# HGRN2 on one Trainium2 core: units paired by feature tile instead of by token half, and started earlier in the projection

## The chip, the cores and the metric

The kernel runs on one core of one Trainium2 chip. The metric is the device time of one execution in microseconds (us), the median of several runs. The engines are TensorE (PE in the rows), VectorE (DVE), ScalarE (ACT) and GpSimd (POOL); SyncE (SP) issues most DMAs.

## What is computed

Two layers of a decoder trunk on 1024 tokens of 1024 features, in fp32. In each layer one input projection feeds four head groups of 256 features each, two of which matter here:

```python
proj = rmsnorm(h, attn_norm_g[i]) @ w_in[i]
y_c = hgrn2_group(hg_q, hg_f, hg_i, lb_all[i])     # gated linear recurrence
y_d = s5_group(s5_u, ...)                          # state space, then a GLU

# hgrn2_group, per head and chunk of tokens
log_f = logaddexp(log(lb), log1p(-lb) + log_sigmoid(z)); k = (1 - lb) * sigmoid(-z)
bcum  = cumsum(log_f)
scores[t, s] = sum_k q[t, k] * k[s, k] * exp(bcum[t, k] - bcum[s, k])     # s <= t
o     = scores @ v + (q * exp(bcum)) @ state
state = exp(b_last) * state + (k * exp(b_last - bcum)).T @ v
```

The other two groups are attention. The groups are normalised, HGRN2's is gated, one output projection and a conv MLP follow.

## The kernel before

Features lie on the 128 partitions, tokens on the free axis in two halves of 512. A 256-feature group is thus two feature tiles (`ft`) by two token halves (`n`). Products in fp32 are made of three matmuls of split operands (`mm3`: L738, L739, L740 in the projection, L726 to L728 elsewhere). A weight tile is split by a cast (L714, ACT or DVE) and a subtraction (L103, DVE or POOL).

**HGRN2** is done in four units (`hgrn_unit`, L256), one for each feature tile and token half, of 15 steps each. A unit makes gates from `z` (L213: ACT's Abs, Exp and Ln, then on DVE `hk` L222, `z` L227, the running sum `hb` L237; in layer 1 also L230, L235, L236), then `kh` (L267, L269), which PE transposes (`khT`, L292). PE makes `pu` (L301) from the transposed `kT` and the values `v`, and DVE adds it to the running state `st` (L306, L308). Then seven levels follow. A level makes `g` (DVE L279, ACT exponentials, DVE L282) and two halves of `qz` (DVE L286); PE makes the scores `psc` (L327), and DVE puts them into `sc` under a mask (L331, L333). An eighth step writes the diagonal (PE L337, DVE L338). At the end PE makes `poh` from `sc`, `v`, `st` and `qb` (L351, L353), and ACT copies it to `yc` (L355). The state runs from token half 0 to token half 1 of one feature tile.

**S5** (`s5`) takes its two feature tiles in turn: DVE, POOL and ACT make matrices (`care`, `caim`, `bare`, `baim`), PE makes `ucp`, `utp` and `sin`, DVE the scans `s5z` (L585 to L609), then PE 24 matmuls into `ys` (L619, L622), and from `ys` come `yt` and the transposed `yf` (L635) and `yl`. A GLU follows: DVE's `zh` (L662), PE's `gl` (L726 to L728), DVE's `gs`, `gt` (L134, L135) and `yd` (L676).

**The projection** (`in_proj`) makes tile after tile in the order uf and z (ahead of the stage), hq, v, z, hq, misc, fq, fk, v, fq, fk, hg, hg, cq, cq, ckv. Each tile takes 8 x 3 matmuls for each token half, with an eviction on DVE (L1533, L1534, L1587) that multiplies by the norm's factor.

**The order.** `weave` (L684) steps generators in turn: each has a count of steps and a span of the stage, and the one whose next step is due earliest goes first. The projection spans 0 to 1, `s5` 0.1 to 0.7, `hgrn` the pair of numbers that is changed here. `hgrn` waits for flags that the projection sets: `h0` when the tiles of feature tile 0 are issued (z, hq, v), `h1` when those of feature tile 1 are. What `weave` issues is then laid on each engine's in-order queue by the tile framework's scheduler, so that the diff alone does not tell where an instruction stands.

Of the kernel before, what the change touches and what calls it, by code (L numbers as in the profile page):

```python
# [38 lines left out]

T = dict(early=(0, 0.2), s5=((0.1, 0.7), (0.1, 0.7)), hgrn=((0.35, 0.92), (0.35, 0.92)), cd=((0.05, 0.85), (0.05, 0.85)), prep=((0.3, 1), (0.3, 1)), b=(0, 1), a=(0.9, 0.95), pre=(7, 9, 11, 13), vals=(5, 6), ahead=3, plv=4, mx=0, pw=1, rt=2, sc=2, rp=6, dl=4, qk=(4, 4), up=5)


class Kern:
# [210 lines left out]
def hgrn_unit(K, layer, ft, n, z, q, v, lbc, st, y):  # L256
# [55 lines left out]
    for li in range(len(LEVELS) + 1):  # L312
        if li < len(LEVELS):
            g, qz = ahead
        if li == T['qk'][layer]:
            qk = K.h(name="qk")
# [491 lines left out]
def rms_steps(K, tiles, gains, out, gates=None):  # L808

    nc = K.nc  # L810
    V = nc.vector
    new = [[] for _ in tiles]
    out.extend(new)
    nm = Norm(K, gains, P * len(tiles), split=False)
    for n in range(2):
        for i, x in enumerate(tiles):
            nm.add(i, n, x[n])
        yield
        nm.scale(n)
        yield  # L820
        for i, x in enumerate(tiles):
            xn, hi, lo = K.h(name="xn"), K.h(F32R, "yh"), K.h(F32R, "yl")
            V.scalar_tensor_tensor(xn, x[n], gains[:, i:i + 1], nm.r(n), op0=ALU.mult, op1=ALU.mult)
            if gates is not None:
                V.tensor_tensor(xn, xn, gates[i][n], op=ALU.mult)
            nc.scalar.copy(hi, xn)
            K.lo(V if i % 2 else nc.gpsimd, lo, xn, hi)
            new[i].append((hi, lo))
        yield
# [39 lines left out]
class Head:  # L869
# [67 lines left out]

    def out(self, ahead=T['ahead']):

# [22 lines left out]
        for qh, kt in [(0, kt) for kt in range(4)] + [(1, kt) for kt in range(8)]:  # L962
# [11 lines left out]
            nc.scalar.activation(pr[:, 0:n], ps[:, 0:n], AF.Exp)  # L974
            K.lo(V if T['plv'] and kt % T['plv'] == T['plv'] - 1 else nc.gpsimd, pl[:, 0:n], pr[:, 0:n], ph[:, 0:n])
            pend.append((qh, kt, n, ph, pl))
# [8 lines left out]
def attention(heads):  # L985
# [13 lines left out]
    for i in range(len(heads)):  # L999
        nxt, pre = get(i + 2), iter(())  # L1000
        mx, vals = (b.max(), b.values()) if b else (iter(()), iter(()))
        for step, _ in enumerate(a.out()):
            for _ in range(2 if step % 2 or step < T['mx'] else 1):
                next(mx, None)
            if step == 6 and nxt:
# [3 lines left out]
                pre = nxt.prep()  # L1009
            if step in T['pre']:  # L1010
                next(pre, None)
            if step in T['vals']:
                next(vals, None)
# [438 lines left out]
def body(ctx, tc, xT, pT, pos, invf, sgn, vecs, prms, dsk, bfs, w_fm, w_misc, w_tm, w_uq, w_ukv, w_glu,  # L1452
         w_outb, w_up, w_down, w_pg, w_ple, out):
    nc = tc.nc
    K = Kern(tc, ctx)
# [45 lines left out]
    steps, lbc = [], K.const([P, 6], F32, "lbc")  # L1501
    ready = {}

    def early():

        for l in range(DEPTH):
            head = K.sm([P, 24], name="s5h", tag="s5h", bufs=2)
            nc.scalar.dma_start(head, prms[l][:, 0:24])
            steps.append(s5_steps(K, head))
            yield  # L1510
        rope_tables(K, pos, cst, tabs)
        K.exp_ln()
        hgrn_lb(K, vec[0][:, V_LB:V_LB + 4], lbc)
        ready["steps"] = True
        yield
        for _ in hgrn_consts(K):
            yield
        ready["consts"] = True
# [3 lines left out]
    for l in range(DEPTH):  # L1522
# [5 lines left out]
        z, hq, hv, hg, fq, fk, fv, misc, cq = ([] for _ in range(9))  # L1528
# [11 lines left out]
        rt = K.sm([P, 8], name="rt", tag="rt", bufs=2)  # L1540
# [57 lines left out]
        yc, yd = [K.two(name="yc") for _ in range(2)], []  # L1598
        yb, ya = ([K.two(name=n) for _ in range(2)] for n in ("yb", "ya"))
        h, ycs, yds, res, heads = [], [], [], {}, []  # L1600
# [11 lines left out]

        def hgrn():
            st = [K.h(name="st") for _ in range(2)]
            while "h1" not in ready or "consts" not in ready:
                yield
            for n in range(2):
                u = [hgrn_unit(K, l, ft, n, z[ft][n], hq[ft][n], hv, lbc, st[ft], yc[ft]) for ft in range(2)]
                for _ in range(HGRN_STEPS):
                    for g in u:  # L1620
                        next(g, None)
                        yield
            while "gates" not in ready:
                yield
            yield from rms_steps(K, yc, gain(2), ycs, gates=hg)
# [18 lines left out]

        pre = [(early(), 12, *T['early'])] if l == 0 else []
        weave(*pre, (s5(), 2 * S5_STEPS + GLU_STEPS + RMS_STEPS, *T['s5'][l]), (hgrn(), 4 * HGRN_STEPS + RMS_STEPS, *T['hgrn'][l]), (in_proj(), IN_STEPS, 0, 1))

        ready["fox"] = True
# [106 lines left out]
        xs, rp = nm.xs, nm.r  # L1755
# [6 lines left out]
        ws, pend, pw = {}, None, {}  # L1762
# [7 lines left out]
        for i, u in enumerate(units + [None]):  # L1770
# [3 lines left out]
            if pend:  # L1774
                n, m, c, v, t = pend
                V.scalar_tensor_tensor(t[:, c], v[:, c], 0.0, t[:, c], op0=ALU.min, op1=ALU.subtract)
                nc.scalar.activation(v[:, c], t[:, c], AF.Exp)
            if u:
                n, m, c = u
# [20 lines left out]
            if pend:  # L1800
                n, m, c, v, t = pend
# [101 lines left out]
```

## Time and profile before

| | |
|---|---|
| median of 3 runs | 3041.83 us (3039.55 to 3045.96) |
| profiled execution, its own time | 3032.95 us |
| its span | 3031.2 us |
| its mean granted TensorE clock | 0.958 of full speed |
| busy in the span | PE 93%, DVE 73%, ACT 47%, POOL 35% |
| projection of layer 0, first hq eviction to last ckv eviction | 62.7 to 426.5 us |
| projection of layer 1 | 1569.6 to 1912.1 us |

All times inside a run are from the profiled execution, in us from the start of its span. A clock of 1.00 in the profile's rows is 2.4 GHz and 0.50 is 1.2 GHz; a share between them is a stretch that held both.

### The profile page before, as it was taken

To read this page: it belongs to the slowest core of one execution; us is meant where nothing else is said; L and a number is where in the kernel's file an instruction comes from. 1 tells how busy PE (TensorE), PEld (TensorE's weight loads), DVE (VectorE), ACT (ScalarE), POOL (GpSimd) and SP (SyncE) were. 2 spreads that over 40 slices of the span, in tenths; PEclk is the share of its full clock that TensorE was granted. 3 is DMA by queue.
4 is the path that set the end of the run, shared out by engine and by line. 5 is a ranking of instruction groups with operands and counts; after the bars stand their busy time and mean duration, and the time that the engine had idled before them with its cause. 6 is when DMAs were issued, how large, how long until landed. Compare 5 with 4: busy or idle time off the path is not lost.

```text
span 3031.2 us, 37112 instructions
## 1 busy us (share of the span) xinstructions
PE 2825.1 (93%) x13346; PEld 2271.9 (75%) x13346; DVE 2208.3 (73%) x3254; ACT 1414.8 (47%) x2383; POOL 1068.9 (35%) x927
## 2 busy tenths in 40 slices
PE   7899799889899999999999888988989999999997
PEld 6777676666688888888787866766767888888886
DVE  6595768777999998242854966878699999953458
ACT  4234446665444444242732453657654444443346
POOL 2521013345422224555523210325453222255544
PEclk9898799899999999999999998999999999999998
DMA  3101011103222225352421010110032222263533
GB/s 125 38 15 49 22 59 35 35 1 132 70 83 84 84 84 172 130 191 92 152 88 36 19 56 28 53 56 1 31 123 90 82 82 82 82 212 98 185 107 129
DMA packets 112136, 249.68 MB, mean 82 GB/s; under 512 B 17488, under 2 KB 20176, under 8 KB 111952
## 3 DMA queue, kind: packets, MB, share of 16 engines
q1 hardware_dynamic: 110512, 246.66, 24.6%
q8 instruction: 105, 1.72, 0.2%
q10 hardware_dynamic: 1440, 0.65, 0.1%
q14 instruction: 79, 0.65, 0.1%
HBM read 197.58 MB, written 48.50 MB: 81 GB/s over the span
## 4 chain that ended last, share of the span: by engine, by line
PE 56%; DVE 21%; issue 7%; ACT 4%; POOL 2%; DMA 1%; SPq 0%; DVEq 0%; POOLq 0%; ACTq 0%
PE up L1320 8%; PE up L1319 8%; PE up L1318 8%; PE dn L1439 5%; PE dn L1440 5%; PE dn L1438 5%; DVE wx L103 1%; PE qk L968 1%; PE pj L738 1%; DVE mx L897 1%; DVE xq L1199 1%; PE pj L739 1%; PE ob L726 1%; PE pj L740 1%; PE ob L727 1%
## 5 line engine op out<-in xcount | busy, mean ns | idle before, releaser
L103 POOL TENSOR_TENSOR wx<-wr,wx 128x512 fp32r<-128x512 f32 (+1 forms) x293 | 485.6, 1670 | 362.2 <-ACT wx L1421 198.1
L1318 PE MATMUL up<-bh,wx 128*128 128x512 f32 x1232 | 482.8, 392 | 12.2 <-ACT wx L1311 12.2
L1319 PE MATMUL up<-bl,wx 128*128 128x512 f32 x1232 | 483.2, 392 | 7.0 <-DVE bl L103 4.0
L1320 PE MATMUL up<-bh,wx 128*128 128x512 f32 x1232 | 483.4, 392 | 6.3 <-DVE wx L103 6.3
L1318 PEld LDWEIGHTS up<-bh,wx 128*128 128x128 f32 x1232 | 233.5, 190 | 61.5 <-ACT wx L1311 13.1
L1439 PE MATMUL dn<-g,wx 128*128 128x512 f32 x704 | 274.1, 389 | 3.8 <-DVE g L103 3.8
L1319 PEld LDWEIGHTS up<-bl,wx 128*128 128x128 f32 x1232 | 233.5, 190 | 57.5 <-DVE bl L103 4.9
L1320 PEld LDWEIGHTS up<-bh,wx 128*128 128x128 f32 x1232 | 233.3, 189 | 56.9 <-DVE wx L103 8.3
L103 POOL TENSOR_TENSOR pl<-pr,ph 128x512 fp32r<-128x512 f32 x144 | 166.2, 1166 | 306.9 <-ACT pr L974 188.2
L1440 PE MATMUL dn<-g,wx 128*128 128x512 f32 x704 | 273.9, 389 | 0.0
L1438 PE MATMUL dn<-g,wx 128*128 128x512 f32 x704 | 273.9, 389 | 0.0
L103 DVE TENSOR_TENSOR g<-g,g 128x512 fp32r<-128x512 f32 x88 | 105.6, 1215 | 202.7 <-ACT g L1420 186.0
L103 POOL TENSOR_TENSOR wx<-wq,wx 128x512 fp32r<-128x512 f32 x44 | 65.1, 1479 | 517.5 <-ACT wx L1311 517.5
L738 PE MATMUL pj<-xs,wx 128*128 128x512 f32 (+1 forms) x512 | 212.3, 415 | 16.4 <-ACT xs L765 7.3
L1421 ACT CAST wx<-wr 128x1024 fp32r<-128x1024 f32 x88 | 92.4, 1050 | 277.9 <-PE dn L1439 255.4
L740 PE MATMUL pj<-xs,wx 128*128 128x512 f32 (+1 forms) x512 | 207.1, 405 | 2.5 <-DVE wx L103 2.5
L739 PE MATMUL pj<-xs,wx 128*128 128x512 f32 (+1 forms) x512 | 208.1, 406 | 1.1 <-DVE xs L766 1.1
L1439 PEld LDWEIGHTS dn<-g,wx 128*128 128x128 f32 x704 | 132.1, 188 | 32.1 <-DVE g L103 4.7
L1440 PEld LDWEIGHTS dn<-g,wx 128*128 128x128 f32 x704 | 132.1, 188 | 27.4
L1438 PEld LDWEIGHTS dn<-g,wx 128*128 128x128 f32 x704 | 132.1, 188 | 27.4
L1329 DVE SCALAR_TENSOR_TENSOR cv<-u,vec,cv 128x1023 f32<-128x1023 f32 x88 | 131.0, 1491 | 28.0 <-ACT cv L1328 27.8
L1330 DVE SCALAR_TENSOR_TENSOR cv<-u,vec,cv 128x1022 f32<-128x1022 f32 x88 | 137.8, 1568 | 0.1
(468 smaller groups left out, 6940.5 us busy)
## 6 DMA issues: line engine op xcount, KB each, us to landing
wr<-in_w_down SPq DMA_DIRECT2D x88, 512.0 KB, 3.5
wr<-in_w_up SPq DMA_DIRECT2D x88, 256.0 KB, 2.9
wq<-in_w_up SPq DMA_DIRECT2D x88, 256.0 KB, 3.9
hid<-cv SPq DMA_DIRECT2D x44, 512.0 KB, 3.3
g<-hid SPq DMA_DIRECT2D x88, 256.0 KB, 5.2
wr<-in_w_fm SPq DMA_DIRECT2D x30, 512.0 KB, 3.9
wr<-in_w_pg SPq DMA_DIRECT2D x28, 512.0 KB, 3.5
hdr<-h SPq DMA_DIRECT2D x48, 256.0 KB, 2.0
```

Source lines behind the costliest of these rows:

```text
L103: eng.tensor_tensor(out, x, hi.bitcast(F32), op=ALU.subtract)
L738: nc.tensor.matmul(out, lhsT=ah, rhs=bh, start=(i == 0), stop=False)
L739: nc.tensor.matmul(out, lhsT=ah, rhs=bl, start=False, stop=False)
L740: nc.tensor.matmul(out, lhsT=al, rhs=bh, start=False, stop=(i == n - 1))
L1318: nc.tensor.matmul(ps, lhsT=ah, rhs=bh, start=k == 0, stop=False)
L1319: nc.tensor.matmul(ps, lhsT=ah, rhs=bl, start=False, stop=False)
L1320: nc.tensor.matmul(ps, lhsT=al, rhs=bh, start=False, stop=k == KD // 2 - 1)
L1329: V.scalar_tensor_tensor(c[:, 1:], u[:, :S - 1], cw[:, 1:2], c[:, 1:], op0=ALU.mult, op1=ALU.add)
L1330: V.scalar_tensor_tensor(c[:, 2:], u[:, :S - 2], cw[:, 0:1], c[:, 2:], op0=ALU.mult, op1=ALU.add)
L1438: nc.tensor.matmul(ps[m], lhsT=ah, rhs=gh, start=f == 0, stop=False)
L1439: nc.tensor.matmul(ps[m], lhsT=ah, rhs=gl, start=False, stop=False)
L1440: nc.tensor.matmul(ps[m], lhsT=al, rhs=gh, start=False, stop=f == NFF - 1)
```

## The change

The loops over token halves and feature tiles inside `hgrn` change places. Before, the first pair of units was token half 0 of both feature tiles and the second pair was token half 1 of both. Now the first pair is both token halves of feature tile 0, which needs the flag `h0` only, and the second pair both halves of feature tile 1. The start of `hgrn`'s span goes from 0.35 to 0.2 in both layers; its end stays at 0.92.

```diff
-T = dict(..., hgrn=((0.35, 0.92), (0.35, 0.92)), ...)
+T = dict(..., hgrn=((0.2, 0.92), (0.2, 0.92)), ...)
...
         def hgrn():
             st = [K.h(name="st") for _ in range(2)]
-            while "h1" not in ready or "consts" not in ready:
-                yield
-            for n in range(2):
-                u = [hgrn_unit(K, l, ft, n, z[ft][n], hq[ft][n], hv, lbc, st[ft], yc[ft]) for ft in range(2)]
+            for ft in range(2):
+                while f"h{ft}" not in ready or "consts" not in ready:
+                    yield
+                u = [hgrn_unit(K, l, ft, n, z[ft][n], hq[ft][n], hv, lbc, st[ft], yc[ft]) for n in range(2)]
                 for _ in range(HGRN_STEPS):
                     for g in u:
                         next(g, None)
                         yield
```

The units and their instructions are the same. What moves is their place on the engines' queues. Three places are shown.

The first is DVE's queue in layer 0 behind the eviction of z's second token half. The numbers at the names are the tiles' own, which differ between the two programs; z_230 and z_231 are the two halves of feature tile 0. Before, the scans of the first S5 tile come next:

```order
L1533 TENSOR_TENSOR z_1044<-pj_1139,rs_344 128x512
L103 TENSOR_TENSOR wx_1507<-wr_1504,wx_1506 128x1024
L585 TENSOR_TENSOR s5z_1242<-sin_1224,phr_1091 128x512
...
L607 TENSOR_TENSOR s5z_1245<-s5z_1245,s5z_1244 128x4x127
L609 TENSOR_TENSOR s5z_1246<-s5z_1246,s5z_1243 128x4x127
L1533 TENSOR_TENSOR hq_1204<-pj_1279,rs_344 128x512
L103 TENSOR_TENSOR wx_1718<-wr_1715,wx_1717 128x1024
L1534 TENSOR_TENSOR misc_1337<-pj_1345,rs_260 68x512
```

Now the first pair's gates, `kh`, two levels of each unit and the state's first copy stand there:

```order
L1533 TENSOR_TENSOR z_1044<-pj_1147,rs_344 128x512
L222 SCALAR_TENSOR_TENSOR hk_1142<-z_230,ha_1141 128x512
L227 SCALAR_TENSOR_TENSOR z_230<-z_230,ha_1141 128x512
...
L237 SCALAR_TENSOR_TENSOR hb_1186<-anew,z_231 128x512
L585 TENSOR_TENSOR s5z_1264<-sin_1246,phr_1091 128x512
...
L609 TENSOR_TENSOR s5z_1268<-s5z_1268,s5z_1265 128x4x127
L267 TENSOR_TENSOR kh_1307<-hb_1186 128x512
...
L286 SCALAR_TENSOR_TENSOR qz_1353<-g_1348,heads,hq_488 128x256 x2
L1533 TENSOR_TENSOR hq_1226<-pj_1313,rs_344 128x512
L306 COPY st_1139<-pu_1401 128x64
```

The work of the first pair has moved ahead into the place between z and misc. On PE's queue `pu_1401`, which the copy reads, stands behind the last `ys` matmul:

```order
L622 MATMUL ys_1370<-caim_784,s5z_1268 128x128
L301 MATMUL pu_1401<-v_697,kT_1331 64x64 x4
L301 MATMUL pu_1401<-v_844,kT_1331 64x64 x4
```

Before, the first `pu` of layer 0 stood more than 100 rows further back, behind the transposes at row 670.

The second place is DVE's queue around the eviction of the second fq tile in layer 0. Before, the second pair's gates stand behind it:

```order
L676 TENSOR_TENSOR yd_2532<-yl_2192,gs_2530 128x512
L1533 TENSOR_TENSOR fq_2485<-pj_2493,rs_260 128x512
...
L222 SCALAR_TENSOR_TENSOR hk_2558<-z_231,ha_2557 128x512
L227 SCALAR_TENSOR_TENSOR z_231<-z_231,ha_2557 128x512
L237 SCALAR_TENSOR_TENSOR hb_2559<-anew,z_231 128x512
```

Now the gates, `kh` and the first unit's first level stand ahead of it:

```order
L222 SCALAR_TENSOR_TENSOR hk_2283<-z_1043,ha_2282 128x512
L227 SCALAR_TENSOR_TENSOR z_1043<-z_1043,ha_2282 128x512
L237 SCALAR_TENSOR_TENSOR hb_2284<-anew,z_1043 128x512
...
L269 TENSOR_TENSOR kh_2512<-kh_2512,hk_2344 128x512
...
L286 SCALAR_TENSOR_TENSOR qz_2585<-g_2580,heads,hq_1225 128x256 x2
L1533 TENSOR_TENSOR fq_2518<-pj_2526,rs_260 128x512
```

The third is PE's queue near the end of the second pair in layer 0. Before, six levels stand in a row, with no projection between them, and the diagonals behind:

```order
L738 MATMUL pj_3121<-xs_138,wx_3117 128x512
L739 MATMUL pj_3121<-xs_139,wx_3117 128x512
L740 MATMUL pj_3121<-xs_138,wx_3118 128x512
L327 MATMUL psc_2977<-qz_2896,g_2891 128x2x64 x4
L327 MATMUL psc_3012<-qz_2923,g_2918 128x2x64 x4
L327 MATMUL psc_3045<-qz_2939,g_2934 128x2x64 x4
L327 MATMUL psc_3054<-qz_2974,g_2969 128x2x64 x4
L327 MATMUL psc_3076<-qz_2988,g_2983 128x2x64 x4
L327 MATMUL psc_3082<-qz_3023,g_3018 128x2x64 x4
L337 MATMUL psc_3107<-heads,qk_2932 128x2 x4
```

Now at most five stand in a row, and they do so 70 rows further ahead, between two groups of 24 projection matmuls:

```order
L740 MATMUL pj_2975<-xs_178,wx_2896 128x512
L798 MATMUL ss_2804<-sq_2758,ones 128x512
L327 MATMUL psc_2822<-qz_2707,g_2702 128x2x64 x4
L327 MATMUL psc_2848<-qz_2755,g_2750 128x2x64 x4
L327 MATMUL psc_2875<-qz_2773,g_2768 128x2x64 x4
L327 MATMUL psc_2912<-qz_2800,g_2795 128x2x64 x4
L327 MATMUL psc_2947<-qz_2833,g_2828 128x2x64 x4
L738 MATMUL pj_3033<-xs_114,wx_3029 128x512
```

The last five levels of the second pair now have 6 to 24 projection matmuls between them. Outside the projection stages of the two layers, PE's queue is the same row for row.

## Rows read from the trace of the kernel before

**Rows 1.** The page's first part (busy time of each engine) and chain.

```profile
PE 2825.1 (93%) x13346; PEld 2271.9 (75%) x13346; DVE 2208.3 (73%) x3254; ACT 1414.8 (47%) x2383; POOL 1068.9 (35%) x927
PE 56%; DVE 21%; issue 7%; ACT 4%; POOL 2%; DMA 1%; SPq 0%; DVEq 0%; POOLq 0%; ACTq 0%
```

**Rows 2.** Busy time of each engine by stretch, both projections and parts of them.

```profile
core 0: us, PE busy (x) PEld busy (x) DVE busy (x) ACT busy (x) POOL busy (x), PEclk, DMA share, GB/s
57.00:425.00 368.00, 328.91 (x1800) 265.69 (x1801) 249.66 (x570) 130.94 (x256) 81.84 (x130) 0.87 0.13 41
116.00:219.00 103.00, 93.47 (x583) 76.45 (x582) 79.31 (x200) 29.79 (x61) 39.81 (x63) 0.92 0.09 24
304.00:425.00 121.00, 103.53 (x479) 79.46 (x480) 79.55 (x132) 46.65 (x92) 12.82 (x12) 0.83 0.15 48
357.00:385.00 28.00, 18.09 (x73) 16.03 (x73) 21.57 (x36) 10.56 (x22) 2.50 (x2) 0.54 0.00 1
1564.00:1912.00 348.00, 311.97 (x1814) 253.70 (x1814) 236.79 (x460) 135.51 (x264) 61.59 (x84) 0.94 0.13 41
1616.00:1715.00 99.00, 88.92 (x557) 71.91 (x555) 74.49 (x161) 30.46 (x61) 36.44 (x59) 0.93 0.08 23
1789.00:1912.00 123.00, 103.45 (x521) 79.41 (x520) 91.48 (x143) 55.71 (x107) 12.35 (x12) 0.93 0.17 54
```

**Rows 3.** What PE waits for in layer 0's projection: total, times, longest.

```profile
PE psc L327 <- DVE qz L286: 14.8, 8, 3.1
```

**Rows 4.** PE's timeline, layer 0: start, busy; idle time ahead and what ended it.

```profile
131.91 0.48 PE L622 MATMUL ys<-care,s5z 64*128 64x128 f32 x2 [1.99 <-DVE s5z L607]
144.79 0.63 PE L622 MATMUL ys<-caim,s5z 64*128 64x128 f32 x2
241.53 1.05 PE L327 MATMUL psc<-qz,g 128*128 128x128 f32 x8
371.67 2.05 PE L327 MATMUL psc<-qz,g 128*128 128x128 f32 x8 [2.51 <-DVE qz L286]
398.76 0.39 PE L740 MATMUL pj<-xs,wx 128*128 128x512 f32 x1
398.99 0.40 PE L738 MATMUL pj<-xs,wx 128*128 128x512 f32 x1
```

**Rows 5.** DVE's timeline, layer 0: start, busy; idle time ahead and what ended it.

```profile
153.15 0.69 DVE L1534 TENSOR_TENSOR misc<-pj,rs 68x512 f32<-68x512 f32 x1 [18.96 <-PE pj L740]
214.74 1.76 DVE L607 TENSOR_TENSOR s5z<-s5z,s5z 128x508 f32<-128x508 f32 x1
304.17 0.68 DVE L1533 TENSOR_TENSOR fq<-pj,rs 128x512 f32<-128x512 f32 x1
323.86 0.87 DVE L286 SCALAR_TENSOR_TENSOR qz<-g,heads,hq 128x256 f32<-128x256 f32 x2
352.61 0.42 DVE L282 TENSOR_TENSOR g<-g,hk 128x256 f32<-128x256 f32 x1
353.74 0.68 DVE L279 TENSOR_TENSOR g<-hb 128x512 f32<-128x512 f32 x1
355.25 1.90 DVE L286 SCALAR_TENSOR_TENSOR qz<-g,heads,hq 128x256 f32<-128x256 f32 x2
357.67 0.70 DVE L333 COPY_PREDICATED sc<-lm,psc 128x512 f32<-128x512 uint8 x1
382.20 1.31 DVE L338 COPY_PREDICATED sc<-mdiag,psc 128x1024 f32<-128x1024 uint8 x1
```

**Rows 6.** DVE's timeline, layer 1.

```profile
1651.49 0.69 DVE L1534 TENSOR_TENSOR misc<-pj,rs 68x512 f32<-68x512 f32 x1 [18.82 <-PE pj L740]
1789.50 0.68 DVE L1533 TENSOR_TENSOR fq<-pj,rs 128x512 f32<-128x512 f32 x1
1813.16 0.87 DVE L286 SCALAR_TENSOR_TENSOR qz<-g,heads,hq 128x256 f32<-128x256 f32 x2
```

**Rows 7.** POOL's timeline, layer 0.

```profile
355.54 1.32 POOL L317 TENSOR_TENSOR qk<-hq,hk 128x512 f32<-128x512 f32 x1 [6.56 <-PE psc L327]
```

More of the change, by code (lines that the diff above doesn't have):

```diff
@@ L37 @@
 NS5 = 24 + 4 * 128
-T = dict(early=(0, 0.2), s5=((0.1, 0.7), (0.1, 0.7)), hgrn=((0.35, 0.92), (0.35, 0.92)), cd=((0.05, 0.85), (0.05, 0.85)), prep=((0.3, 1), (0.3, 1)), b=(0, 1), a=(0.9, 0.95), pre=(7, 9, 11, 13), vals=(5, 6), ahead=3, plv=4, mx=0, pw=1, rt=2, sc=2, rp=6, dl=4, qk=(4, 4), up=5)
+T = dict(early=(0, 0.2), s5=((0.1, 0.7), (0.1, 0.7)), hgrn=((0.2, 0.92), (0.2, 0.92)), cd=((0.05, 0.85), (0.05, 0.85)), prep=((0.3, 1), (0.3, 1)), b=(0, 1), a=(0.9, 0.95), pre=(7, 9, 11, 13), vals=(5, 6), ahead=3, plv=4, mx=0, pw=1, rt=2, sc=2, rp=6, dl=4, qk=(4, 4), up=5)
 class Kern:
```

## Prediction, made before the changed kernel ran

> **What bounds the kernel now.** I read the page first. PE is busy 93% of the span and holds most of the chain, with DVE second [rows 1]: the kernel is bound by PE wherever PE has its operands, and time can only be won where it waits or runs below full clock. Then the stretches [rows 2]. In the two projections, the only part where the change moves anything, PE is busy 328.9 of 368 us at a mean clock of 0.87 and 312.0 of 348 us at 0.94. The reader is to see in the same rows that DVE is busy two thirds of these stretches: neither engine is full, they wait for each other in turn.
>
> The stretch from 357 to 385 us is the worst. PE is busy 18.1 of 28 us at a clock of 0.54 [rows 2], and the list of PE's waits puts 14.8 us on the levels of HGRN2, that is on `qz` [rows 3]. In the order these are the six levels that stand in a row. The timeline shows one: PE stands 2.51 us for `qz`, then makes a level in 2.05 us, where the same level took 1.05 us at full clock [rows 4]. DVE makes the next `qz` meanwhile, so the two engines alternate.
>
> The opposite lies earlier. DVE stands idle 18.96 us before the eviction of misc in layer 0 and 18.82 us in layer 1 [rows 5, 6], while HGRN2 has not begun. From 116 to 219 us, up to the last scans of the second S5 tile (L607 at 214.74), DVE is idle 103 - 79.3 = 23.7 us; in layer 1, from 1616 to 1715, 99 - 74.5 = 24.5 us [rows 2, 5].
>
> **The change, part by part.** No instruction is added or removed, so the sum is over places.
>
> *The second pair's head leaves the tail.* I call the eviction of the second fq tile F: it is at 304.17 and 1789.50 us [rows 5, 6]. Before, the second pair's gates, `kh` and first level come behind F, and the first `qz` is there at 323.86, 19.7 us after F; in layer 1 at 1813.16, 23.7 us after. In the new order they stand ahead of F in layer 0, and the gates do in layer 1. So PE finds levels ready at once. What PE still has to do behind F in layer 0, counted in the new order: 333 projection and GLU matmuls at 0.23 us (the distance of two starts at full clock, 398.76 and 398.99 [rows 4]) = 76.6; 14 levels at 1.05 = 14.7 [rows 4]; 66 smaller rows, which at the same 0.23 would be 15 and which have a quarter of the columns or fewer for the most part, so I take 10. Together 101 us, with bounds of 95 and 106. The stretch from F to 425 takes 121 us now [rows 2], so it ends 20 us nearer to F. Layer 1 in the same way: 323 x 0.23 + 14.7 + 10 = 99 against 123 us, 24 nearer. DVE is no bound there: it needs 79.6 us of the 121 now, less some 9 that move out.
>
> *Where F comes to stand.* That is the open term. Ahead of the second S5 tile's last scans the new order has more of the first pair. From the order, between z's eviction and that L607, layer 0: 6 more `g`, 6 L282, 6 pairs of `qz`, 10 L333, 2 diagonals and one half of a weight subtraction (priced as a `g`). Layer 1: 8, 8, 8, 12, 2 and 1. By their rows (0.68, 0.42, 0.87, 0.70, 1.31 [rows 5]) that is 6 x 1.97 + 7.0 + 2.6 + 0.7 = 22 us and 8 x 1.97 + 8.4 + 2.6 + 0.7 = 27.5 us. DVE's idle time there is 23.7 and 24.5 us, so the moved work just fits in, if all of it can be filled. Not all can: the state's first copy (L306) waits for `pu`, which stands on PE behind the 24 `ys`, and these took from 131.91 to 145.42 us at low clock [rows 4]. Ahead of the copy DVE has gates, `kh` and two units' first level to do, so of the 18.96 us I take 12 as filled and 7 as left. Then 23.7 - 7 = 17 us take in 22, and the second S5 tile comes 5 us late in layer 0, and 27.5 - 17.5 = 10 us late in layer 1. The bounds are 0 (all filled; a few us early if PE's own waits in that stretch go too) and 22 and 27.5 (nothing filled).
>
> Behind the second S5 tile the way to F gets shorter, since the first pair's last levels are done ahead of it now, and the second pair's gates and `kh` (9 us of DVE work) fall into a stretch in which DVE waits for the GLU anyway. In layer 0 I take the 5 us as regained: F stays. In layer 1 the new order also has 55 more PE matmuls ahead of F (30 of a `poh`, 12 of the GLU, a level, diagonals), about 10 us at the prices above, which lie beside the 10 us late; I take F as 12 us later.
>
> *The wait added.* PE's projection behind fq now needs a bank that DVE frees behind the second pair's gates and `kh`; I expect PE to stand some us there, and for `kh` ahead of `khT`, in place of the waits that it has there now. Behind it all the rest of the projection stands. It is within the 101 us' bounds.
>
> The sum: 20 us in layer 0 and 24 - 12 = 12 us in layer 1, **32 us less**. Against the profiled execution (3032.95 us) that is 3001; that execution lies 8.9 us below the median of the runs, so carried to the median it is **3010 us**. For the whole of it: with F 10 us earlier in layer 0 and unmoved in layer 1 it would be 30 + 24 = 54 us less, 2988.
>
> **The rivals.** *Late S5 (slower).* If DVE fills none of its idle time, since it stands at the state's copies behind `ys` as long as it stood before, F comes 22 us late in layer 0 and 27.5 in layer 1, and up to 5 later there for the PE rows moved ahead. The layers then end 2 and up to 8.5 us later than before: about 3052. It decides as soon as the two delays of F together exceed 20 + 24 = 44 us. For it speaks that `pu` stands behind `ys` in the order; against it that some 7 us of gates and levels stand ahead of the copy, in idle time.
>
> *A slower DVE.* The first pair's levels now run where POOL works: POOL is busy 39.8 of the 103 us from 116 to 219, and 36.4 of 99 in layer 1 [rows 2]. A pair of `qz` took 1.90 us at 355.25, beside a POOL instruction of 1.32 us that began at 355.54, where the pair at 323.86 took 0.87 [rows 5, 7]. If half of the 14 pairs in each layer pay the 1.03 us, F comes 7 us later in both: 18 us less than before, 3024. If all pay and the score copies too, it is near nothing.
>
> The Trainium skill has the rule to this (SBUF — State Buffer, the section on who interferes with whom): a VectorE instruction with two inputs in SBUF and a GpSimd instruction that reads SBUF take turns at a port, and the second one waits until the first is done. The slow pair at 355.25 agrees with it in sign. By the rule the price of a clash would be what is left of a POOL instruction, and at most POOL's 39.8 and 36.4 us.
>
> *No gain.* PE's loss behind F (121 - 101 = 20, and 24 us) comes back elsewhere: it waits at F's bank and at `khT`, its clock falls there, and the levels are as far apart as DVE makes them. Then the time is that of before, 3042. For it speaks that PE is at 0.87 and 0.94 of full clock over the whole projections [rows 2], so that low clock follows every wait; against it that at most five levels stand in a row now, with 24 projection matmuls behind them.
>
> **How the numbers follow.** The forecast with its better side has 0.60 (its own range is 2988 to 3026), the slower DVE 0.13 (most of it still faster), no gain 0.11, late S5 0.16. A measurement of this kernel can tell some 0.2%, 6 us. Faster by more: 0.60 and 0.13 of the second, 0.73. Within: 0.11. Slower: 0.16. The range is 2988 to 3050: it reaches into the late S5, whose end is 3052, and leaves out a tenth there and about 0.05 below.
>
> **What would show it.** After the change the idle time before misc should be about 7 us for 19, ended by `pu` or `ys` at the copy L306; the second S5 tile's L607 near 219 and 1720; F near 304 and 1801; the first `qz` of the second pair before F or at it; no stretch in which six levels alternate at half clock, and the window of the tail at a clock above 0.8; the last ckv eviction near 406 and, from layer 1's own start, 12 us earlier. Everything outside the two projections should take as long as before. Wrong would be the prediction if F moved by more than 10 us in layer 0, if POOL slowed the levels, or if the 99 and 101 us behind F held waits of PE of more than 5 us.

## The result, and the profile after

The changed kernel takes 3021.11 us (median of 4 runs, 3013.74 to 3024.58), the kernel before 3040.69 us (4 runs): a ratio of 0.9937, 95% interval 0.9922 to 0.9952, so 19 us less. Forecast were 3010 us and 32 us less, within 2988 to 3050. The profiled execution took 3013.74 us with a span of 3012.0 us, 19.2 us shorter than the span of before.

First the marks of the two projections. DVE's timeline of the changed kernel (start, busy; idle time ahead and what ended it), layer 0 and then layer 1:

```profile
62.91 0.69 DVE L1533 TENSOR_TENSOR hq<-pj,rs 128x512 f32<-128x512 f32 x1 [2.34 <-PE pj L740]
119.88 1.63 DVE L237 TENSOR_TENSOR_SCAN hb<-anew,z 128x512 f32<-128x512 f32 x1
150.36 0.23 DVE L306 COPY st<-pu 128x64 f32<-128x64 f32 x1 [6.02 <-PE pu L301]
231.23 1.75 DVE L607 TENSOR_TENSOR s5z<-s5z,s5z 128x508 f32<-128x508 f32 x1
284.44 1.22 DVE L237 TENSOR_TENSOR_SCAN hb<-anew,z 128x512 f32<-128x512 f32 x1
309.72 0.68 DVE L1533 TENSOR_TENSOR fq<-pj,rs 128x512 f32<-128x512 f32 x1
366.72 1.31 DVE L338 COPY_PREDICATED sc<-mdiag,psc 128x1024 f32<-128x1024 uint8 x1
408.61 0.68 DVE L1533 TENSOR_TENSOR ckv<-pj,rs 128x512 f32<-128x512 f32 x1
...
1553.19 0.69 DVE L1533 TENSOR_TENSOR hq<-pj,rs 128x512 f32<-128x512 f32 x1 [5.21 <-PE pj L740]
1713.16 1.75 DVE L607 TENSOR_TENSOR s5z<-s5z,s5z 128x508 f32<-128x508 f32 x1
1789.46 0.68 DVE L1533 TENSOR_TENSOR fq<-pj,rs 128x512 f32<-128x512 f32 x1
1892.65 0.68 DVE L1533 TENSOR_TENSOR ckv<-pj,rs 128x512 f32<-128x512 f32 x1
```

The last ckv evictions of the kernel before; the second line holds two evictions in a row, and the last of them began at 1911.46:

```profile
425.86 0.68 DVE L1533 TENSOR_TENSOR ckv<-pj,rs 128x512 f32<-128x512 f32 x1
1910.86 1.27 DVE L1533 TENSOR_TENSOR ckv<-pj,rs 128x512 f32<-128x512 f32 x2
```

Against [rows 5, 6] and the stage starts of the table, 62.74 and 1569.55: layer 0's projection, from the start of the first hq to the start of the last ckv eviction, went from 363.1 to 345.7 us, layer 1's from 341.9 (1569.55 to 1911.46) to 339.5. Layer 0 gave 17 us of the 19.2, layer 1 about 2. The rest between and behind the two stages is unchanged within a microsecond: 1143.7 and 1144.6 us between them.

Then the stretches of the changed kernel (PE busy, PEld, DVE, ACT, POOL, granted clock, DMA), which stand beside [rows 2]:

```profile
62.91:409.30 346.39, 303.39 (x1782) 245.52 (x1781) 253.01 (x553) 134.05 (x259) 87.24 (x130) 0.93 0.13 41
1553.19:1893.30 340.11, 305.17 (x1782) 248.84 (x1781) 231.10 (x458) 136.91 (x265) 63.19 (x84) 0.92 0.12 40
1789.46:1892.65 103.19, 94.78 (x479) 74.40 (x480) 74.44 (x127) 46.35 (x89) 12.89 (x12) 0.91 0.15 52
...
116.00:235.00 119.00, 109.42 (x715) 86.91 (x714) 105.65 (x234) 34.11 (x73) 47.60 (x66) 0.96 0.11 35
235.00:309.70 74.70, 55.07 (x292) 44.47 (x291) 37.54 (x51) 39.92 (x71) 6.34 (x4) 0.86 0.11 36
309.72:408.61 98.89, 90.87 (x455) 70.77 (x456) 71.96 (x120) 43.85 (x83) 13.73 (x12) 0.94 0.16 54
360.00:388.00 28.00, 27.07 (x146) 18.75 (x145) 13.36 (x18) 12.50 (x22) 2.88 (x2) 1.00 0.18 58
```

The same two stages of the kernel before, first hq to last ckv, and between them its stretch from F to the last ckv of layer 0:

```profile
62.74:426.50 363.76, 324.67 (x1782) 262.18 (x1781) 247.89 (x553) 130.56 (x254) 81.84 (x130) 0.87 0.12 39
304.17:425.86 121.69, 104.39 (x483) 80.16 (x484) 79.99 (x133) 47.34 (x93) 12.82 (x12) 0.83 0.15 48
1569.55:1912.10 342.55, 306.52 (x1790) 249.25 (x1789) 236.55 (x459) 135.51 (x263) 61.59 (x84) 0.94 0.13 40
```

The reader is to see where layer 0's gain lies. PE does not wait less: it is idle 363.76 - 324.67 = 39.1 us before and 346.39 - 303.39 = 43.0 us after. The same 1782 matmuls are busy 21 us less, at a mean clock of 0.93 instead of 0.87. Of these 21 us 13.5 lie behind F (104.39 us busy before, 90.87 after). There the window of the six levels, 28 us at 0.54 before, has its counterpart at 360 to 388 us, at 1.00; the five levels that stand in a row now come ahead of that window and take 1.29 us each, more than the 1.05 at full clock.

The other 8 lie ahead of F. There one group of matmuls, S5's 96 `ys`, gives 12 us, and others lose 4 again. PE's time for them (PE busy, granted clock of the whole stretch, DMA) from the stage's start to F, first before and then after:

```profile
62.74:304.17 241.43, 28.30 (x96) 0.89 0.11 34
62.91:309.72 246.81, 16.36 (x96) 0.92 0.12 36
```

Before, PE waited 1.99 us inside the first set [rows 4] and the rest of it ran at half clock for the most part. In the change PE waits 3.93 us ahead of it, for `khT`, 22 projection matmuls run behind that wait, and the `ys` behind them run at 1.00.

PE's waits have moved to the stretch ahead of F too: from F to the last ckv PE is idle 8.0 us for 17.3, ahead of F 35 us for 22. Its timeline shows what the prediction called the wait added, and the row of five levels:

```profile
132.92 1.09 PE L292 MATMUL khT<-ident,kh 128*128 128x128 f32 x4 [3.93 <-DVE kh L269]
291.93 1.11 PE L292 MATMUL khT<-ident,kh 128*128 128x128 f32 x4 [2.17 <-DVE gs L134]
301.37 0.69 PE L292 MATMUL khT<-ident,kh 128*128 128x128 f32 x4 [2.77 <-DVE kh L269]
307.25 1.12 PE L301 MATMUL pu<-v,kT 128*64 128x64 f32 x16 [5.19 <-ACT kT L294]
310.46 0.79 PE L738 MATMUL pj<-xs,wx 128*128 128x512 f32 x1 [2.08 <-DVE fq L1533]
335.65 6.43 PE L327 MATMUL psc<-qz,g 128*128 128x128 f32 x40
```

In layer 1 the same place holds one wait of 10.48 us, at 1790.20, for the eviction of fq at 1789.46.

### The profile page after: what moved, and what is told of

It is laid out like the page before. It is cut to its first block, busy times and chain, and to the rows that moved or that the text cites. A ratio compares the mean times of both kernels' runs of the same rounds, so it can differ in the third digit from the quotient of the medians.

```text
span 3012.0 us, 37104 instructions
## 1 busy us (share of the span) xinstructions
PE 2800.0 (93%) x13346; PEld 2254.1 (75%) x13346; DVE 2208.6 (73%) x3254; ACT 1415.5 (47%) x2383; POOL 1075.6 (36%) x927
## 4 chain that ended last, share of the span: by engine, by line
PE 58%; DVE 26%; issue 7%; ACT 5%; POOL 3%; DMA 1%; SPq 0%; DVEq 0%; ACTq 0%; POOLq 0%
PE up L1320 8%; PE up L1319 8%; PE up L1318 8%; PE dn L1439 5%; PE dn L1440 5%; PE dn L1438 5%; DVE wx L103 2%; PE pj L738 2%; PE pj L739 2%; PE pj L740 2%; PE qk L968 1%; DVE xq L1199 1%; DVE qz L286 1%; PE ob L726 1%; DVE mx L897 1%
## 5 line engine op out<-in xcount | busy, mean ns | idle before, releaser
L738 PE MATMUL pj<-xs,wx 128*128 128x512 f32 (+1 forms) x512 | 216.5, 423 | 28.0 <-DVE fq L1533 12.6
L739 PE MATMUL pj<-xs,wx 128*128 128x512 f32 (+1 forms) x512 | 209.6, 409 | 1.0 <-DVE xs L766 1.0
L740 PE MATMUL pj<-xs,wx 128*128 128x512 f32 (+1 forms) x512 | 208.3, 407 | 1.4 <-DVE wx L103 1.4
L1438 PEld LDWEIGHTS dn<-g,wx 128*128 128x128 f32 x704 | 132.2, 188 | 27.5
L738 PEld LDWEIGHTS pj<-xs,wx 128*128 128x128 f32 (+1 forms) x512 | 99.8, 195 | 55.7 <-DVE fq L1533 13.2
```

What stands on the lines that cost most here:

```text
L738: nc.tensor.matmul(out, lhsT=ah, rhs=bh, start=(i == 0), stop=False)
L739: nc.tensor.matmul(out, lhsT=ah, rhs=bl, start=False, stop=False)
L740: nc.tensor.matmul(out, lhsT=al, rhs=bh, start=False, stop=(i == n - 1))
L1438: nc.tensor.matmul(ps[m], lhsT=ah, rhs=gh, start=f == 0, stop=False)
```

## The experiments

All ratios are against the kernel before, with 95% intervals; a thousandth is 3 us.

### The loops alone

```diff
 # changed kernel
-hgrn=((0.2, 0.92), (0.2, 0.92))
+hgrn=((0.35, 0.92), (0.35, 0.92))
```

> The new loops (both token halves of one feature tile) with the old start of the span, 0.35. My theory: the gain is the second pair's gates, kh and first level standing ahead of the second fq eviction (F). In this order they stand behind it, as in the kernel before, and eight levels stand in a row on PE, so the time should be that of before: 3041 us, within 6. Rival, the pairing itself is what helps (less to wait for, one state per pair): 3021 us, the time of the changed kernel.

Measured: 1.0004 (0.9990 to 1.0018). The loops alone, from 0.35, do nothing. This fits my theory, but also any theory in which the span does the work.

### The span alone

```diff
 # kernel before
-hgrn=((0.35, 0.92), (0.35, 0.92))
+hgrn=((0.2, 0.92), (0.2, 0.92))
```

> The old loops with the span from 0.2; the first pair still waits for the second feature tile's z and hq. In the order the first pair moves ahead by some 50 rows of PE, the second pair's gates still stand behind F, and five levels stand in a row at the end, some 50 rows later than before. My theory: no head of the second pair ahead of F, so the stretch from F to the last ckv eviction stays near 120 us and the time within 8 us of 3041. Rival, the longer span alone spreads the levels and takes PE's waits out: about 3021 us.

Measured: 0.9962 (0.9948 to 0.9977), 12 us less; my theory had no gain. The projections themselves became as short as in the changed kernel or shorter: layer 0 takes 343.6 us (64.64 to 408.20), layer 1 336.1 (1559.11 to 1895.25). PE still waits in the tail of layer 0, but three times in place of a row of six, as its timeline shows:

```profile
360.36 2.04 PE L327 MATMUL psc<-qz,g 128*128 128x128 f32 x8 [3.05 <-DVE qz L286]
364.92 2.05 PE L327 MATMUL psc<-qz,g 128*128 128x128 f32 x8 [2.51 <-DVE qz L286]
370.53 2.04 PE L327 MATMUL psc<-qz,g 128*128 128x128 f32 x8 [3.56 <-DVE qz L286]
```

Part is given back outside: from the last ckv of layer 0 to the first hq of layer 1 it takes 1150.9 us instead of 1143.7, and from the last ckv of layer 1 to the end of the span 1129.7 instead of 1119.7. HGRN2's last diagonals come 32 us ahead of the last ckv in layer 0, 44 before.

### The new loops, waiting for both tiles

```diff
 # changed kernel
-                while f"h{ft}" not in ready or "consts" not in ready:
+                while "h1" not in ready or "consts" not in ready:
```

> The changed kernel, but its first pair waits for both feature tiles (h1) as the old loops do. My theory: the pairing by feature tile does nothing of its own; it only lets the first pair start ahead of the second tile's z and hq, in the time in which DVE stands idle ahead of misc. Then this is the time of the old loops with the span from 0.2, 11 to 12 us below before: 3028 us, and DVE stands idle some 19 us ahead of misc again. Rival, pairs of one feature tile and one state are better in themselves (a pair of its own has less to wait for): 3021 us or less, the time of the changed kernel.

Measured: 0.9951 (0.9935 to 0.9966), 15 us less. That lies between the span alone (0.9962) and the change (0.9937), and its interval holds both, so neither the pairing's share of the 19 us nor that of the earlier start of the first pair is settled. The profiles show what the earlier start trades. Here the projections are shorter than in the change, 342.7 and 332.3 us for 345.7 and 339.5, but between them it takes 1155.2 us for 1144.6 and behind them 1129.5 for 1119.4, so 21 us are given back outside, as 17 are with the span alone and none in the change. HGRN2's last diagonals come 30 and 23 us ahead of the last ckv here, 39 and 41 in the change; that this is the cause is not shown.

One thing this run does settle. DVE's timeline of this kernel:

```profile
154.68 0.69 DVE L1534 TENSOR_TENSOR misc<-pj,rs 68x512 f32<-68x512 f32 x1 [20.34 <-PE pj L740]
```

The idle time ahead of misc is all there, 20.34 us, and the kernel is still 15 us faster than before. Filling DVE's idle time, on which the prediction's account of F rests, is not what the gain needs.

### The second pair's head alone

```diff
 # kernel before; u[0], u[1] are the two pairs
-    dec = K.sm([P, 4], name="dec")
+    dec = K.sm([P, 4], name="dec", tag="dec", bufs=4)
...
+            head = 3 if l == 0 else 4
+            for n in [0] * 9 + [1] * head + [0] * (HGRN_STEPS - 9) + [1] * (HGRN_STEPS - head):
+                for g in u[n]:
+                    next(g, None)
+                    yield
```

> The kernel before (old loops, 0.35) with the second pair's gates and kh issued during the first pair's sixth-last to last steps, so that they stand ahead of F in both layers, as in the changed kernel (dec gets buffers of its own). The first pair is not earlier, and five levels still stand in a row at the end of the tail. If the second pair's head ahead of F is what shortens the tail, as my prediction had it: some 20 us less in a layer, 3005 to 3020 us. Rival, formed after the runs with one part of the change alone: the head does nothing without room for the levels, which comes from the first pair in DVE's early idle time; then F comes later by what is put ahead of it and the time is 3041 us or more.

Measured: 1.0013 (1.0003 to 1.0022), no gain. The gates of the second pair stand well ahead of F here (the running sums at 246.4 and 265.1 us, F at 310.2). From F to the last ckv eviction layer 0 takes 114.9 us, 7 less than before, and F itself comes 5 us later. In layer 1 the stretch takes 127.0 us, 5 more than before, and F comes 7 us later. The head was the first term of the prediction's sum; alone it brings nothing.

### Layer 0 alone

```diff
 # changed kernel: new loops and 0.2 if l == 0, else the old loops and 0.35
+hgrn=((0.2, 0.92), (0.35, 0.92))
```

> The change in layer 0 alone; layer 1 keeps the old loops and 0.35, and layer 1's queues are those of the kernel before. In the profiles layer 0's projection became 17.4 us shorter and layer 1's 2.5 us. If the layers add, this is 17 us below before, 3024 us, and layer 1's projection takes 341.9 us from its first hq eviction to its last ckv eviction, as before. Rival, each layer holds half of the gain and the split in one profile is chance of the clock: 3031 us.

Measured: 0.9958 (0.9941 to 0.9974), 13 us less. Between the two expectations: layer 0 holds about two thirds of the 19 us, though the two intervals overlap. In its profile layer 0's projection is 347.9 us (17 expected less, 15 found), but layer 1's, with the queues of the kernel before, takes 348.5, and not 341.9. In the kernel with the loops alone it takes 351.0. So the profile of before seems to have caught a short layer 1 (that execution lies 8 us below the median of its kernel), and the 2 us that layer 1 seems to gain there are too few. Where the difference arises, the last section shows.

### S5 earlier

```diff
 # changed kernel
-s5=((0.1, 0.7), (0.1, 0.7))
+s5=((0.1, 0.6), (0.1, 0.6))
```

> The changed kernel with S5's span ending at 0.6 instead of 0.7. The second S5 tile's last scans (L607) then stand some 23 DVE rows further ahead in layer 0 and 8 in layer 1, with its transposes 109 and 86 PE rows further ahead. My theory: F came 5.5 us late in layer 0 and 16 us late in layer 1 because that S5 tile stood behind the first pair's levels on DVE. So F should come back by 5 to 10 us in each layer, and the time be 3005 to 3012 us. Rival, F is set by PE's own work and clock, and the S5 chain has slack: 3021 us. A third outcome, HGRN2's first pair is pushed back by as much and the tail grows again: above 3021 us.

Measured: 0.9849 (0.9824 to 0.9874), 46 us less than before and 27 less than the change. The gain is larger than expected, and in this profile it is PE's waiting. The two stages of this kernel:

```profile
63.78:404.30 340.52, 311.65 (x1782) 252.15 (x1781) 249.32 (x553) 132.90 (x258) 81.40 (x130) 0.91 0.13 41
1549.72:1876.80 327.08, 304.03 (x1782) 246.30 (x1781) 230.01 (x458) 137.19 (x265) 64.41 (x84) 0.94 0.13 41
```

PE is idle 28.9 and 23.1 us, where the changed kernel has 43.0 and 34.9; it is busy 8 us more in layer 0 and 1 us less in layer 1. S5's second L607 comes 157 and 144 us after the stage's start, for 168 and 160. F comes 250 and 230 us after it, for 247 and 236: in layer 1 earlier as expected, in layer 0 later, so F is not the gauge that I took it for.

Four neighbours tell how far this goes. The same S5 span with the kernel before:

```diff
 # kernel before
-s5=((0.1, 0.7), (0.1, 0.7))
+s5=((0.1, 0.6), (0.1, 0.6))
```

> The kernel before (old loops, 0.35) with S5's span ending at 0.6 alone. If most of the 46 us of the earlier-S5 version come from S5 alone, whatever HGRN2 does: 3015 us. If it works only together with an early HGRN2 pair (my theory: S5 earlier leaves HGRN2's second pair where it was, five levels in a row at the end of the tail, so PE waits there as before): 3030 us or more.

Measured: 1.0040 (1.0024 to 1.0057), 12 us slower. And with the old loops and the span from 0.2:

```diff
 # kernel before
-s5=((0.1, 0.7), (0.1, 0.7)), hgrn=((0.35, 0.92), (0.35, 0.92))
+s5=((0.1, 0.6), (0.1, 0.6)), hgrn=((0.2, 0.92), (0.2, 0.92))
```

> Old loops (token half 0 of both tiles first), span from 0.2, S5's span to 0.6: the earlier-S5 version but for the loops. If the pairing by feature tile does nothing of its own once S5 is early: 2996 us, the time of that version. My theory now, from the run with the old loops and 0.2: the first pair starts later since it waits for the second tile, the second pair ends later, and its products are still to be done when the projection is over; that cost 16 us outside the two projections: 3010 us.

Measured: 0.9993 (0.9978 to 1.0008), no gain, worse than either expectation. Its profile gives back 20 us outside the two projections, 9 between them and 12 behind them, where 16 were expected. So the early S5 pays with the new loops and the early start together and not with the old loops, whichever start they have; with the new loops from 0.35 it was not run. Beside it the loops, with the earlier flag that comes with them, are worth 44 us, where they seemed to do little. Then S5's span to 0.5 on the changed kernel:

```diff
 # changed kernel
-s5=((0.1, 0.7), (0.1, 0.7))
+s5=((0.1, 0.5), (0.1, 0.5))
```

> The changed kernel with S5's span ending at 0.5. In the order the second S5 tile's last scans stand another 19 DVE rows ahead in layer 0, but HGRN2's first pair ends later. If S5's chain to the second fq eviction still sets the time: 2985 us. If HGRN2's first pair is now as late as S5 was: 2996 us, no further gain, or some us more.

Measured: 0.9948 (0.9928 to 0.9968), no better than the change; HGRN2's first diagonals start 210 and 212 us after layer 0's stage start, for 149 and 152 in the change. And to 0.65:

```diff
 # changed kernel
-s5=((0.1, 0.7), (0.1, 0.7))
+s5=((0.1, 0.65), (0.1, 0.65))
```

> The changed kernel with S5's span ending at 0.65, between 0.7 (20 us below before) and 0.6 (46 us below). The second S5 tile's last scans stand at DVE row 435 in layer 0, between 448 and 425. If the delay of S5 behind the first pair sets the time step by step: 3005 to 3012 us. If 0.6 is one lucky interleaving: anything, and not between the two.

Measured: 0.9942 (0.9925 to 0.9959). That is the time of 0.7, not one between 0.7 and 0.6. The step at 0.6 is real, since a second kernel with 0.6 shows it too (below), but it is not a steady effect of S5's delay; what in the interleaving at 0.6 makes it is open.

### The state update later

```diff
 # changed kernel, in hgrn_unit: the block from pu = K.px("pu") to the last st, moved into the loop over levels
+        if li == 2:
+            pu = K.px("pu")
...
         if li == 5:
```

> The changed kernel with the state update of a unit (pu on PE, the six copies and sums on DVE) issued three levels later. DVE stood idle 6.02 us at the first of these copies in layer 0, behind the 24 ys matmuls. My theory: without that wait the second S5 tile's scans come up to 6 us earlier in layer 0 and some us in layer 1, and with them the second fq eviction: 3012 us. Rival, the wait only moves to the scores, which stand behind the same ys on PE: 3021 us.

Measured: 0.9920 (0.9901 to 0.9940), some 5 us less than the change, with intervals that overlap. S5's second L607 in layer 0 comes 167.0 us after the stage's start for 168.3, so hardly earlier. The wait at the state's copy is gone, but DVE waits nearly as long a little earlier, for ACT's exponentials of a level:

```profile
149.31 0.65 DVE L282 TENSOR_TENSOR g<-g,hk 128x256 f32<-128x256 f32 x1 [5.54 <-ACT g L280]
```

That is in kind what the rival said, that the wait only moves. With S5's span to 0.6 as well:

```diff
 # kernel with the later state update
-s5=((0.1, 0.7), (0.1, 0.7))
+s5=((0.1, 0.6), (0.1, 0.6))
```

> S5's span to 0.6 and the state update three levels later, both on the changed kernel. If the two act on different waits: 46 us below before and 3 to 5 more, 2990 us. If the later state update only takes out a wait that the earlier S5 has removed: 2996 us.

Measured: 0.9831 (0.9817 to 0.9846), a median of 2988.43 us: 51 us below before, the fastest version. Beside the same kernel without the later update (0.9849) it is again some 5 us. Both times the intervals overlap, so that the later update brings anything is not clear of the noise.

## Why the prediction was right, and where it was not

The time was in the range and on the forecast side, the size was off by 11 us, and the mechanism was not the one named.

**The stretch behind F** came out near its size, and that was in good part luck. Forecast were 101 and 99 us behind F. Measured from F to the last ckv: 408.61 - 309.72 = 98.9 us in layer 0, for 121.7 before, and 1892.65 - 1789.46 = 103.2 in layer 1, for 122.0. But the sum does not describe what PE did there. It counted 333 and 323 projection and GLU matmuls. The trace has 240 in either layer, all of the projection (PE busy, granted clock, DMA):

```profile
309.72:408.61 98.89, 61.01 (x240) 0.94 0.16 54
1789.46:1892.65 103.19, 63.75 (x240) 0.91 0.15 52
```

PE is ahead of DVE's evictions: the GLU and three groups of 24 projection matmuls that stand behind F's own matmuls in layer 0's order were done when DVE evicted F. At the prediction's 0.23 us the 93 and 83 missing matmuls are 21 and 19 us. Their place was taken by what the sum did not have: 8.0 and 8.4 us in which PE is idle, a clock of 0.94 and 0.91 instead of 1.00, and more small matmuls than the 66 counted. More than 5 us of waits there was one of the prediction's own signs of being wrong.

**Where F comes to stand** was the term that missed. Counted from the stage's start, F came 5.5 us later in layer 0 (246.8 for 241.4), forecast 0, and 16 us later in layer 1 (236.3 for 220.0), forecast 12. Together 10 of the 12 us that the profiles fall short of the forecast 32 are here; 5 more are in layer 1's stretch behind F, and layer 0's gave 3 back. The steps inside it show why. The wait at the state's copy was there as forecast, 6.02 us for 7, ended by `pu`. But S5's second L607 came 16 us late in layer 0 and 19 in layer 1, forecast 5 and 10. Three things were missing in layer 0. DVE filled 12 us of idle time, not 17: of the time from z's second eviction to that L607 it was idle 23.7 us before and 11.7 after. Of the ten score copies (L333) that moved ahead, all priced at 0.70 us, four took 1.30 to 1.34, which is 2.4 us. These are the last two of a unit's six copies, and they take this in both kernels, also where POOL is idle. A row of DVE and the next of POOL in the change, then a row of DVE in the kernel before, where POOL is idle from 219 to 244 us:

```profile
195.81 1.31 DVE L333 COPY_PREDICATED sc<-lm,psc 128x512 f32<-128x512 uint8 x1
200.75 1.42 POOL L343 TENSOR_TENSOR qb<-qb,hq 128x512 f32<-128x512 f32 x1 [17.27 <-ACT qb L342]
...
241.02 1.32 DVE L333 COPY_PREDICATED sc<-lm,psc 128x512 f32<-128x512 uint8 x1 [0.67 <-PE psc L327]
```

And DVE became slower beside POOL, which was the rival that I gave 0.13. The running sum at 119.88, with POOL busy, took 1.63 us, the one at 284.44, with POOL idle, took 1.22. The row of POOL beside the first:

```profile
118.84 1.59 POOL L394 TENSOR_TENSOR s5t<-phi 128x252 f32<-128x252 f32 x1
```

POOL was busy 47.6 of the 119 us. Over the groups of instructions that both orders have between z's eviction and that L607, the score copies aside, each count at its mean duration of before, the durations grew by 4 us. The Trainium skill's rule (SBUF — State Buffer, on who interferes with whom) fits the sign, but no run took POOL's work away, so that POOL is the cause is read from rows standing side by side and not shown by an experiment. The three make up the 16 us: 22 us of moved work, 2.4 and 4 more, less the 12 filled. In layer 1 10 us were filled, not 17.5, the score copies cost the same 2.4, and the other durations did not grow. Behind L607 layer 0's way to F was 78.5 us for 89.4, so 11 us were regained where I took 5.

**The mechanism that failed** is "the second pair's head leaves the tail". With the head ahead of F and the span as before, the time stayed (1.0013). With the span from 0.2 and the head behind F, it fell by 12 and 15 us. So the head is neither enough nor needed for most of the gain; whether it adds some us beside the longer span is not settled, since the intervals overlap. What these two share with the change, and the head alone lacks, is the longer span: HGRN2's 66 steps lie over 0.72 instead of 0.57 of the projection's 68, so 0.74 projection steps instead of 0.59 pass for each, and the first pair begins earlier. Which of the two, the wider spacing or the earlier start, makes the gain was not taken apart. The profiles say how it shows: the row of six levels at half clock is gone or broken up, and in the change layer 0's gain is in busy time and not in the sum of PE's waits: 13.5 us behind F, and 12 in the `ys`, for which the prediction had no term, less 4 that other matmuls ahead of F lose. The `ys` are not what the gain needs either: with the span alone and with the first pair waiting for both tiles layer 0's 96 `ys` take 28.3 and 28.4 us, as before.

**The rivals.** Late S5 happened for the most part (16 and 19 us of the 22 and 27.5), and did not decide, since the way behind it became shorter. The slower DVE happened to some 4 us, in layer 0. No gain is what layer 1 looks like in one profile, though less in the runs: layer 0 alone gives 13 of the 19 us. The reason given for it, that low clock follows every wait, is not what the rows show: the last section has a wait of 2.92 us with a clock of 1.00 behind it. A rival that came up in the runs, that the loops do nothing of their own, is not refuted with S5's span to 0.7, and with 0.6 the loops together with their earlier flag matter.

## What to carry to other kernels

Where work is interleaved by due times, moving one stream's span shifts every other stream in the in-order queues, so what one span is worth depends on the others: S5's earlier end cost 12 us before this change and brought 27 us after it. Try them together before the first is judged. And look at busy time and clock beside the waits: a change can leave PE's idle time as it is and still gain, if fewer of its matmuls run at half clock, and these need not be the ones that were aimed at. Last, an order gives each engine's own queue and not how far one engine is ahead of another: here PE had done some 90 of the matmuls counted behind F when DVE evicted F.

## What the runs showed of the hardware

The same queue, with the same waits, can meet a different clock. Layer 1 of the kernel before and of the kernel with layer 0 alone have the same rows on PE. Ahead of the second `ys` matmuls PE waits twice in both, 2.92 and 1.89 us before, 2.91 and 1.86 in the other. Up to there the two run alike, each matmul within 0.3 us of the other from the stage's start. The kernel before, PE's timeline:

```profile
1709.42 1.13 PE L327 MATMUL psc<-qz,g 128*128 128x128 f32 x8 [2.92 <-DVE qz L286]
1714.58 0.46 PE L619 MATMUL ys<-tz,ut 128*128 128x128 f32 x2 [1.89 <-issue]
```

its stretch behind the first wait, with the second in it (columns as above):

```profile
1709.50:1719.50 10.00, 8.11 (x54) 6.85 (x55) 10.00 (x15) 2.17 (x6) 4.49 (x3) 1.00 0.00 0
```

And the kernel with layer 0 alone:

```profile
1695.19 1.13 PE L327 MATMUL psc<-qz,g 128*128 128x128 f32 x8 [2.91 <-DVE qz L286]
1700.32 0.60 PE L619 MATMUL ys<-tz,ut 128*128 128x128 f32 x2 [1.86 <-issue]
```

and its stretches from the same place on:

```profile
1695.30:1705.30 10.00, 8.14 (x43) 6.84 (x44) 10.00 (x16) 2.17 (x6) 3.33 (x2) 0.76 0.00 0
1705.30:1715.30 10.00, 10.00 (x34) 7.53 (x34) 3.59 (x6) 2.20 (x7) 1.31 (x1) 0.50 0.00 0
```

In the first the granted clock stays at 1.00, in the second it falls to 0.50, 1.2 GHz, and the first pair's diagonals come 193.4 us after the stage's start instead of 185.5. In the kernel with the loops alone these 48 `ys` ran at 0.50 as well, 14.9 us for 8.5 in the kernel before. That is 8 us between two executions of the same rows at one place, of which 7 are left at the stage's end, four tenths of what this change is worth. What tips the clock there no row shows. It means that a difference between two single profiles has to be held against the intervals of the runs.
